# Sliding-window attention with the transposed probabilities as the stationary operand

## The chip, the core and the metric

The kernel runs on one NeuronCore of a Trainium2 chip. Five engines have instruction queues of their own: TensorE (PE, matmuls and transposes into PSUM), VectorE (DVE), ScalarE (ACT), GpSimd (POOL) and SyncE (SP, DMA issue). The metric is the device time of one execution, in microseconds, as the median of several runs.

## What is computed

Two layers over 1024 tokens of width 1024, all in float32. The first has two head groups behind one input projection: sliding-window softmax attention (8 query heads of 64, 2 key/value heads, window 128, a learned sink per head) and four DeltaNet heads. The second is a gated linear recurrence. Each mixer and each squared-relu MLP is followed by a layer norm. The part that the change touches is this one, per block of 128 queries and its band of 256 keys:

```
s = jnp.einsum('bnqhgd,bnkhd->bnhgqk', qb, kb).astype(f32) * (DH ** -0.5)
...
s = jnp.where(mask[None, :, None, None], s, -jnp.inf)
...
p = jax.nn.softmax(jnp.concatenate([s, sink], axis=-1), axis=-1)[..., :-1]
o = jnp.einsum('bnhgqk,bnkhd->bnqhgd', p.astype(v.dtype), vb)
```

## The kernel before

The tokens are two streams of 512 (c = 0 and 1), each in four blocks of 128 (n). Large products are made from split operands: every float32 matrix is written as a high part (fp32r, tiles `h`, `wh`) and a low part (`l`, `wl`), and `mm3` issues three matmuls. Their PSUM tiles are named `mm` (four banks). Everything small, such as attention, DeltaNet and the transposes of the layer norm, uses tiles named `mx` (four other banks). ACT and DVE make the high and low parts of the weights (`wblock`), which arrive in `ws`. `proj_fm` has weights stationary and activations moving (in the order `mm<-g,wh`), `proj_tm` the reverse.

The order on TensorE is fixed while the kernel is built, by a planner in Python (`Clock`, and the loop at the end of `trunk`). It keeps a planned time for every engine. The two streams yield the large products, and small chains (`attention`, `attn_preps`, `head_mid`, `layernorm`, called mixers) are put between them as soon as their operands are ready by the planned times. `Clock.matmul` charges a float32 matmul with 4 x 0.42 ns for each moving column, whatever the stationary operand is. `PE.last` chains all TensorE instructions, so their order on the chip is exactly the planned one. Instructions on the other engines are ordered by the compiler's scheduler.

`attn_block` handles one block n. It makes the scores (`mx<-kT,g`) with queries on partitions, adds the mask and takes the maximum (DVE), and exponentiates in place with the sum in `den` (ACT). Then it multiplies each of the eight probability tiles by one over its sum (ACT), transposes them on TensorE in groups of four, copies each group out of PSUM to `pT`, and multiplies: `v` (64 columns) is stationary, `pT` (512 columns) moves. One such product stands behind each group of transposes. The output already has channels on partitions and goes into `oT` through `split_ps`. The first block of stream 0 has one key tile instead of two.

Three conditions of the planner matter below. `attention` holds two granules of the pool `g` (`slot`) until the last block of stream 1 is done. `mix_out` of a stream (output projection, then layer norm) needs free granules, and its layer norm needs four more before its transposes are planned. And `mlp` chooses, at every second eighth of the hidden width, between two ways for W2: `straight` (eight products of quarter matrices for each fourth of the hidden width) and `weave`/`seven` (seven products, with sums of W2's quarters made earlier by DMA); stream 0 stays with `straight` until the output projection of stream 1 has been planned:

```
while e < 8 and not ((c == 1 or sts[1].get("op", -1) >= layer) and rings["g"] >= 2 and e % 2 == 0):
    if e == 7:
        res["start"]()
    yield from straight(e, e == 7)
    e += 1
```

Of the kernel before, what the change touches and what calls it, by code (L numbers as in the profile page):

```python
# [12 lines left out]
AF = mybir.ActivationFunctionType  # L13
ALU = mybir.AluOpType
# [3 lines left out]
P = 128  # L18
# [195 lines left out]
def trunk(ctx: ExitStack, tc, I, out):  # L214
    nc = tc.nc
    clk = Clock(tc, nc)
    V, G, S, PE = clk.engine(nc.vector, "V"), clk.engine(nc.gpsimd, "G"), clk.engine(nc.scalar, "S"), clk
    DS, DA, DG = clk.engine(nc.sync, "V"), clk.engine(nc.scalar, "V"), clk.engine(nc.gpsimd, "V")
    at = lambda *a: lambda: clk.ready(*a)
# [12 lines left out]
    def nm(s):  # L232
        uid[0] += 1
        return f"{s}_{uid[0]}"
# [34 lines left out]
    def wait(cond):  # L269
        while not cond():  # L270
            yield BLOCK
# [4 lines left out]
    def mx_ps():  # L276
        return clk.tile("mx", 4, pmx.tile([P, 512], F32, tag="mx", name=nm("mx")))

    def v4(a):
        return a.rearrange("p (a b) -> p a b", a=4)  # L280

    def bc_last(a, n):
        return a.unsqueeze(2).to_broadcast([P, a.shape[1], n])
# [9 lines left out]
    ident, U, M1 = C["ident"], C["U"], C["M1"]  # L293
# [100 lines left out]
    def split_ps(h, l, ps):  # L394
        S.copy(h, ps)
        V.tensor_tensor(l, ps, h, ALU.subtract)
# [419 lines left out]
    def attn_block(c, n, st, oT, tl, o):  # L816
        vr = st["v"][n]
        yield from wait(lambda: "ok" in o)
        qT, kT = o["qT"], o["kT"]
        pk, pv = att["kT"], att["v"]  # L820
        keys = ([(pk, pv)] if pk is not None else []) + [(kT, vr)]
        att["kT"], att["v"] = kT, vr
        k0 = 2 - len(keys)
        w = len(keys) * P
        sc = cpool.tile([P, 40], F32, tag="asc", name=nm("asc"), bufs=2)
        mx, nmx, den, es = (sc[:, i * 8:(i + 1) * 8] for i in range(4))
        pm = []
        for gp in range(2):
            yield lambda: max(clk.ready(qT, kT), clk.bank("mx", 4, 2))
            ps = [mx_ps().rearrange("p (g k) -> p g k", g=2) for _ in range(2)]  # L830
            for g2 in range(2):
                g = 2 * gp + g2
                for i, (kk, _) in enumerate(keys):
                    for h in range(2):
                        PE.matmul(ps[h][:, g2, i * P:(i + 1) * P], qT[h * 64:(h + 1) * 64, g * P:(g + 1) * P],
                                  kk[h * 64:(h + 1) * 64, :], start=True, stop=True)
            for h in range(2):
                pt = tl[2 + 2 * gp + h].rearrange("p (g k) -> p g k", g=2)
                for g2 in range(2):
                    i = 2 * (2 * gp + g2) + h  # L840
                    V.tensor_tensor_reduce(pt[:, g2, :w], ps[h][:, g2, :w], C["amask"][:, k0 * P:], 1.0, NEG,
                                           ALU.add, ALU.max, mx[:, i:i + 1])
                pm.append(pt)
        V.scalar_tensor_tensor(nmx, mx, -0.125, nsink, ALU.mult, ALU.min)
        V.tensor_tensor(es, W["sinks"], nmx, ALU.add)
        for m in range(4):
            for g2 in range(2):
                i = 2 * (2 * (m // 2) + g2) + m % 2
                S.activation(pm[m][:, g2, :w], pm[m][:, g2, :w], AF.Exp, bias=nmx[:, i:i + 1], scale=0.125,
                             accum_out=den[:, i:i + 1])  # L850
        S.activation(es, es, AF.Exp)
        V.tensor_tensor(den, den, es, ALU.add)
        V.reciprocal(den, den)
        for m in (0, 2, 1, 3):
            for g2 in range(2):
                i = 2 * (2 * (m // 2) + g2) + m % 2
                S.activation(pm[m][:, g2, :w], pm[m][:, g2, :w], AF.Copy, scale=den[:, i:i + 1])
        yield at(*pm)
        po = mx_ps()
        pend = None  # L860
        for i, (_, vv) in enumerate(keys):
            for h in range(2):
                ps = mx_ps()
                for g in range(4):
                    PE.transpose(ps[:, g * P:(g + 1) * P], pm[2 * (g // 2) + h][:, g % 2, i * P:(i + 1) * P], ident)
                pT = tl[(6, 7, 2, 3)[2 * i + h]]
                (S.copy if h else V.tensor_copy)(pT, ps)
                yield at(pT)
                PE.matmul(po[h * 64:(h + 1) * 64, :], vv[:, h * 64:(h + 1) * 64], pT, start=(i == 0),
                          stop=(i == len(keys) - 1))  # L870
        h, l = oT.quad(0, n)
        split_ps(h, l, v4(po))
        yield lambda: 0.0


# [377 lines left out]
    def attention(c, st, oT, o):  # L1253
        for n in range(NT):
            yield from attn_block(c, n, st, oT, slot["tl"], o[n])
            st["att"] = n + 1
        if c == 1:
            free("g", *slot["g"])
# [143 lines left out]
    while streams or mixers:  # L1402
        m = next((m for m in mixers if m[0]() + MARGIN <= clk.now), None) if clk.bank("mx", 4) <= clk.now else None
# [144 lines left out]
```

## Time and profile before

| | us |
|---|---|
| median of 3 runs (2270.96 to 2272.14) | 2271.65 |
| the profiled execution | 2273.03 |
| span of its instructions | 2271.3 |
| TensorE busy | 2210.8 (97%) |
| DVE busy | 1546.5 (68%) |
| ACT busy | 1049.1 (46%) |

The span runs from the first to the last instruction; 1.7 us of the profiled execution lie around it. Attention runs from about 100 to 440 us of the span. The output projection of stream 0 ends at 443 us, and from then to about 490 us its layer norm runs beside the DeltaNet chains of stream 1. The first product of `seven` starts at 803.9 us.

### The profile page before, as it was taken

What the parts mean: (1) busy time and instruction counts of PE and PEld (TensorE: products, weight loads), DVE (VectorE), ACT (ScalarE), POOL (GpSimd) and SP (SyncE); (2) the same over time, 40 slices, a digit from 0 to 9 for tenths busy, and PEclk for the clock granted to TensorE, in tenths of its full rate; (3) what the DMA queues carried; (4) which work ended last, traced back from release to release, by engine and by line L of the source; (5) the groups of instructions that cost most, each with busy time, mean ns of one, the idle gap of its engine ahead of it and who ended that gap; (6) DMA issues with size and microseconds to landing.
All of it is one profiled execution on the core that took longest, in us unless ns stands there. A gap on an engine that the chain in (4) does not pass through costs nothing.

```text
span 2271.3 us, 31951 instructions
## 1 busy us (share of the span) xinstructions
PE 2210.8 (97%) x12436; PEld 1787.7 (79%) x12436; DVE 1546.5 (68%) x2809; ACT 1049.1 (46%) x1878; POOL 28.9 (1%) x56
## 2 busy tenths in 40 slices
PE   8999999979999999999999999999999999999997
PEld 7767877757878887888888878778788887888886
DVE  7787776576555567586567898685565657776477
ACT  5465456244422344454444677373434444444442
POOL 0000000000000000000000000000000000000000
PEclk9999999999999999999999999999999999999999
DMA  4121223256677666677775333323523443444341
GB/s 168 59 78 39 94 77 115 81 171 185 192 200 225 207 215 199 208 255 222 232 216 184 130 130 129 122 75 102 181 98 127 140 144 128 150 169 145 122 165 66
DMA packets 89944, 337.46 MB, mean 149 GB/s; under 512 B 9920, under 2 KB 10304, under 8 KB 81600
## 3 DMA queue, kind: packets, MB, share of 16 engines
q1 hardware_dynamic: 76688, 280.56, 35.7%
q0 software_dynamic: 4608, 33.56, 7.8%
q10 hardware_dynamic: 8496, 21.30, 2.7%
q8 instruction: 97, 1.59, 0.3%
q14 instruction: 55, 0.45, 0.1%
HBM read 324.37 MB, written 78.12 MB: 177 GB/s over the span
## 4 chain that ended last, share of the span: by engine, by line
PE 86%; DVE 8%; ACT 4%; DMA 1%; issue 1%; SPq 0%; ACTq 0%; DVEq 0%
PE mm L206 67%; PE mx L206 17%; DVE g L178 2%; PE mx L210 2%; DVE wl L178 1%; DVE s L178 1%; ACT g L178 1%; DVE t L178 1%; DVE f L178 1%; ACT s L178 1%; ACT wh L178 1%; DMA parked<-r 1%; ACT t L178 1%; ACT f L178 0%; DMA f<-parked 0%
## 5 line engine op out<-in xcount | busy, mean ns | idle before, releaser
L206 PE MATMUL mm<-g,wh 128*128 128x512 f32 x2816 | 883.7, 395 | 2.4 <-ACT g L178 1.2
L178 DVE TENSOR_TENSOR wl<-ws,wh 128x1024 fp32r<-128x1024 f32 (+1 forms) x444 | 538.9, 1214 | 395.7 <-ACT wh L178 391.0
L178 ACT CAST wh<-ws 128x1024 fp32r<-128x1024 f32 (+1 forms) x356 | 371.4, 1043 | 685.2 <-PE mm L206 587.0
L206 PEld LDWEIGHTS mm<-g,wh 128*128 128x128 f32 x2816 | 520.3, 188 | 110.0 <-DVE g L178 3.1
L206 PE MATMUL mm<-g,wl 128*128 128x512 f32 x1408 | 549.6, 390 | 0.0
L206 PE MATMUL mm<-wh,s 128*128 128x512 f32 x1152 | 376.9, 394 | 0.7 <-DVE g L178 0.7
L206 PEld LDWEIGHTS mm<-g,wl 128*128 128x128 f32 x1408 | 264.6, 188 | 55.8
L206 PEld LDWEIGHTS mm<-wh,s 128*128 128x128 f32 x1152 | 217.0, 188 | 46.5 <-ACT s L178 1.1
L206 PE MATMUL mm<-wh,g 128*128 128x512 f32 (+1 forms) x768 | 239.7, 383 | 6.4 <-ACT wh L178 6.2
L206 PE MATMUL mm<-wl,s 128*128 128x512 f32 x576 | 225.1, 391 | 0.0
L206 PE MATMUL mx<-wh,s 128*128 128x512 f32 x576 | 188.0, 392 | 1.2 <-DVE s L178 1.2
L206 PEld LDWEIGHTS mm<-wh,g 128*128 128x128 f32 x768 | 142.9, 191 | 33.4 <-ACT wh L178 6.2
L178 ACT CAST s<-g 128x512 fp32r<-128x512 f32 x172 | 104.7, 622 | 105.5 <-PE mm L206 53.5
L178 DVE TENSOR_TENSOR s<-g,s 128x512 fp32r<-128x512 f32 x172 | 116.4, 688 | 45.0 <-ACT s L178 44.9
L206 PE MATMUL mm<-wl,g 128*128 128x512 f32 (+1 forms) x384 | 144.1, 375 | 0.4 <-DVE wl L178 0.4
L206 PEld LDWEIGHTS mx<-wh,s 128*128 128x128 f32 x576 | 108.2, 188 | 24.0 <-DVE s L178 2.0
L206 PEld LDWEIGHTS mm<-wl,s 128*128 128x128 f32 x576 | 108.6, 189 | 21.4 <-issue 0.2
L206 PE MATMUL mx<-wl,s 128*128 128x512 f32 x288 | 112.2, 390 | 0.0
L178 DVE CAST wh<-ws 128x1024 fp32r<-128x1024 f32 x88 | 60.5, 688 | 69.2 <-PE mm L206 62.4
L178 DVE TENSOR_TENSOR g<-g,mm 128x512 f32<-128x512 f32 x136 | 89.4, 684 | 13.4 <-PE mm L206 12.8
L178 ACT ACTIVATE g<-mm 128x512 f32<-128x512 f32 x100 | 59.1, 591 | 77.0 <-PE mm L206 77.0
L206 PEld LDWEIGHTS mm<-wl,g 128*128 128x128 f32 x384 | 73.3, 191 | 11.8 <-DVE wl L178 0.7
(234 smaller groups left out, 2397.3 us busy)
## 6 DMA issues: line engine op xcount, KB each, us to landing
ws<-w SPq DMA_DIRECT2D x232, 512.0 KB, 3.3
ws<-t SPq DMA_DIRECT2D x96, 512.0 KB, 3.4
t<-w POOLq DMA_DIRECT2D x32, 1024.0 KB, 9.0
ws<-hin_fm SPq DMA_DIRECT2D x32, 512.0 KB, 3.3
t<-w SPq DMA_DIRECT2D x16, 1024.0 KB, 7.1
t<-t SPq DMA_DIRECT2D x16, 1024.0 KB, 7.3
ws<-rin SPq DMA_DIRECT2D x32, 512.0 KB, 3.3
ws<-hout SPq DMA_DIRECT2D x16, 512.0 KB, 3.5
```

Source lines behind the costliest of these rows:

```text
L178: r = f(*a, **k)
L206: ins = self.pe.matmul(out, lhsT, rhs, start=start, stop=stop, skip_group_check=fresh)
L210: return self._pe(self.pe.transpose(out, x, ident), out, [x], 0.00042 * 2 * out.shape[-1])
```

## The change

The eight scalings of the probabilities on ACT are dropped. For each key/value head, the probabilities are transposed for both key tiles, and all four groups are copied out (`pT[i, h]`). Then, in one group of sixteen matmuls, 128 transposed probabilities of one query head are stationary and the 64 columns of `v` move; the output has query rows on partitions. One DVE instruction multiplies it by one over the sum (`y`), four transposes bring it to channels on partitions, and `split_ps` reads those.

```diff
-        for m in (0, 2, 1, 3):
-            for g2 in range(2):
-                i = 2 * (2 * (m // 2) + g2) + m % 2
-                S.activation(pm[m][:, g2, :w], pm[m][:, g2, :w], AF.Copy, scale=den[:, i:i + 1])
-        yield at(*pm)
-        po = mx_ps()
-        pend = None
-        for i, (_, vv) in enumerate(keys):
-            for h in range(2):
+        pT = {}
+        for h in range(2):
+            yield at(pm[h], pm[2 + h])
+            for i in range(len(keys)):
                 ps = mx_ps()
                 for g in range(4):
                     PE.transpose(ps[:, g * P:(g + 1) * P], pm[2 * (g // 2) + h][:, g % 2, i * P:(i + 1) * P], ident)
-                pT = tl[(6, 7, 2, 3)[2 * i + h]]
-                (S.copy if h else V.tensor_copy)(pT, ps)
-                yield at(pT)
-                PE.matmul(po[h * 64:(h + 1) * 64, :], vv[:, h * 64:(h + 1) * 64], pT, start=(i == 0),
-                          stop=(i == len(keys) - 1))
+                pT[i, h] = tl[(6, 7, 2, 4)[2 * h + i]]
+                (S.copy if i else V.tensor_copy)(pT[i, h], ps)
+                yield lambda: 0.0
+        yield at(*pT.values())
+        po = mx_ps()
+        for g in range(4):
+            for h in range(2):
+                o = po[:, (2 * g + h) * 64:(2 * g + h + 1) * 64]
+                for i, (_, vv) in enumerate(keys):
+                    PE.matmul(o, pT[i, h][:, g * P:(g + 1) * P], vv[:, h * 64:(h + 1) * 64], start=(i == 0),
+                              stop=(i == len(keys) - 1))
+        y = tl[3]
+        V.tensor_tensor(y.rearrange("p (i d) -> p i d", i=8), po.rearrange("p (i d) -> p i d", i=8), bc_last(den, 64),
+                        ALU.mult)
+        yield at(y)
+        ps = mx_ps()
+        for g in range(4):
+            PE.transpose(ps[:, g * P:(g + 1) * P], y[:, g * P:(g + 1) * P], ident)
         h, l = oT.quad(0, n)
-        split_ps(h, l, v4(po))
+        split_ps(h, l, v4(ps))
         yield lambda: 0.0
```

Since the planner sets the order, it moves other work too. In the rows below, a tile's name is followed by its number, `x4` counts equal instructions, and the output stands left of `<-`. TensorE, last attention block of stream 1, before (`csb` holds the identity, so those rows are transposes; `mm` rows are the output projection of stream 0):

```order
L206 MATMUL mx_4687<-g_147,vraw_3099 64x512
L210 MATMUL mx_4704<-csb,g_146 128x128 x2
L210 MATMUL mx_4704<-csb,g_147 128x128 x2
L206 MATMUL mm_4629<-wh_4671,g_1135 128x512
L206 MATMUL mm_4629<-wl_4672,g_1135 128x512
L206 MATMUL mm_4629<-wh_4671,g_1136 128x512
```

The same place in the changed kernel:

```order
L210 MATMUL mx_4400<-csb,g_146 128x128 x2
L210 MATMUL mx_4400<-csb,g_147 128x128 x2
L210 MATMUL mx_4406<-csb,g_146 128x128 x2
L210 MATMUL mx_4406<-csb,g_147 128x128 x2
L206 MATMUL mx_4412<-t_3404,t_3405 128x128
L206 MATMUL mx_4412<-t_3404,t_3447 128x128
L206 MATMUL mm_4164<-wh_4366,g_1363 128x512
L206 MATMUL mm_4164<-wl_4367,g_1363 128x512
L206 MATMUL mm_4164<-wh_4366,g_1365 128x512
```

The products with `v` no longer alternate with the transposes: sixteen of them (`mx_4423<-vraw_3055,g_147 128x64` and its like) follow three matmuls further down.

TensorE, layer norm of stream 0 (`mx<-csb,g` are its transposes, `mx<-t_4413` with 32x32 the DeltaNet chain of a head of stream 1), before:

```order
L206 MATMUL mx_5142<-t_4413 32x32 x16
L206 MATMUL mx_5161<-t_4413 32x32 x16
L210 MATMUL mx_5179<-csb,g_4291 128x128 x4
L206 MATMUL mx_5189<-t_4413 32x32 x16
L210 MATMUL mx_5208<-csb,g_4291 128x128 x4
L210 MATMUL mx_5218<-csb,g_4291 128x128 x4
L206 MATMUL mx_5225<-t_4413 32x32 x16
L210 MATMUL mx_5243<-csb,g_4291 128x128 x4
L206 MATMUL mm_5265<-g_4818,wh_5261 128x512
```

The layer norm of stream 0 in the changed kernel:

```order
L210 MATMUL mx_4930<-csb,g_4156 128x128 x4
L210 MATMUL mx_4940<-csb,g_4156 128x128 x4
L206 MATMUL mm_4914<-g_2041,wh_4910 128x512
L206 MATMUL mm_4914<-g_2042,wh_4910 128x512
L206 MATMUL mm_4914<-g_2041,wl_4911 128x512
L210 MATMUL mx_4950<-csb,g_4156 128x128 x4
L210 MATMUL mx_4978<-csb,g_4157 128x128 x4
```

Large products of stream 1 now stand between the transposes, and the 32x32 steps of the DeltaNet chain all come after them. From the end of the output projection to the last transposes of this layer norm the order has 96 large matmuls, seven 32x32 groups of sixteen and four other DeltaNet groups before, and 108 large matmuls, no 32x32 group and three other DeltaNet groups now.

TensorE, first MLP of stream 0: the first W2 product after those of the first two fourths of the hidden width (the rows ahead of it end a hidden block), before:

```order
L206 MATMUL mm_7876<-g_4821,wh_7872 128x512
L206 MATMUL mm_7876<-g_4820,wl_7873 128x512
L206 MATMUL mx_7903<-wh_7911,s_7905 128x512
L206 MATMUL mx_7903<-wl_7912,s_7905 128x512
L206 MATMUL mx_7903<-wh_7911,s_7906 128x512
```

The same product's beginning in the changed kernel:

```order
L206 MATMUL mm_7797<-g_4790,wh_7793 128x512
L206 MATMUL mm_7797<-g_4789,wl_7794 128x512
L206 MATMUL mm_7827<-wh_7833,s_7369 128x512
L206 MATMUL mm_7827<-wl_7834,s_7369 128x512
L206 MATMUL mm_7827<-wh_7833,s_7370 128x512
```

The output of W2 goes to an `mm` bank instead of an `mx` bank: `straight` stands where `seven` stood. Over the whole program TensorE has 32 transposes and 120 matmuls of 128x64 more, 30 products with `v` of 64x512 fewer, and 24 large matmuls more, since the third fourth of stream 0's first MLP is made with eight products (192 matmuls) instead of seven (168). In two stretches the order of TensorE is the same as before: the one that took about 880 to 1320 us in the trace before, and all from about 1606 us to the end.

## Rows read from the trace of the kernel before

**Rows 1.** Page, parts 1 and 2: busy time, and clock in 40 slices.

```profile
PE 2210.8 (97%) x12436; PEld 1787.7 (79%) x12436; DVE 1546.5 (68%) x2809; ACT 1049.1 (46%) x1878; POOL 28.9 (1%) x56
...
PE   8999999979999999999999999999999999999997
...
PEclk9999999999999999999999999999999999999999
```

**Rows 2.** Windows: stretch, its length, busy time of each engine, granted clock, DMA.

```profile
core 0: us, PE busy (x) PEld busy (x) DVE busy (x) ACT busy (x) POOL busy (x), PEclk, DMA share, GB/s
110.00:443.00 333.00, 323.44 (x2577) 240.69 (x2577) 233.90 (x674) 178.21 (x515) 0.60 (x6) 1.00 0.24 80
...
458.00:497.00 39.00, 27.02 (x371) 20.32 (x370) 33.47 (x64) 19.71 (x34) 0.00 (x0) 0.87 0.53 183
...
790.00:880.00 90.00, 90.00 (x398) 74.58 (x398) 52.64 (x60) 38.06 (x51) 3.29 (x4) 1.00 0.71 222
...
1320.00:1606.00 286.00, 278.46 (x1238) 228.43 (x1237) 211.19 (x320) 166.36 (x253) 0.20 (x2) 0.99 0.33 115
```

**Rows 3.** Waits of PE, 0 to 520 us: total us, times, longest.

```profile
PE mx L206 <- DVE t L178: 10.9, 6, 3.9
PE mm L206 <- ACT wh L178: 6.2, 1, 6.2
```

**Rows 4.** Timeline of PE, 440 to 512 us: start, length, what, idle before.

```profile
475.36 0.51 PE L206 MATMUL mx<-t 32*32 32x32 f32 x32 [2.61 <-DVE t L178]
479.76 0.65 PE L206 MATMUL mx<-t 32*32 32x32 f32 x32 [3.90 <-DVE t L178]
480.34 1.11 PE L210 MATMUL mx<-csb,g 128*128 128x128 f32 x4
...
486.73 0.50 PE L206 MATMUL mm<-g,wh 128*128 128x512 f32 x1 [1.17 <-ACT g L178]
```

**Rows 5.** Timeline of DVE, 430 to 488 us: the layer norm of stream 0.

```profile
441.15 1.37 DVE L178 SCALAR_TENSOR_TENSOR g<-g,mm 128x512 f32<-128x512 f32 x2 [1.73 <-PE mm L206]
...
463.26 1.90 DVE L178 TENSOR_TENSOR g<-g,s 128x512 f32<-128x512 f32 x3
...
473.21 0.69 DVE L178 TENSOR_TENSOR g<-g,s 128x512 f32<-128x512 f32 x1
...
476.41 1.22 DVE L178 TENSOR_TENSOR wl<-ws,wh 128x1024 fp32r<-128x1024 f32 x1
477.54 0.29 DVE L178 TENSOR_TENSOR t<-t,mx 128x128 f32<-128x128 f32 x1
```

**Rows 6.** Timeline of PE, 112 to 135 us.

```profile
117.75 1.07 PE L206 MATMUL mx<-g,vraw 128*64 128x512 f32 x2
118.76 0.66 PE L210 MATMUL mx<-csb,g 128*128 128x128 f32 x4
119.25 0.61 PE L206 MATMUL mx<-t,t 128*128 128x128 f32 x4
...
122.44 0.67 PE L206 MATMUL mx<-s,s 64*64 64x64 f32 x8
123.05 1.07 PE L206 MATMUL mx<-g,vraw 128*64 128x512 f32 x2
124.05 0.49 PE L206 MATMUL mx<-t,t 128*128 128x128 f32 x2
```

**Rows 7.** Timeline of PE around 31.6 us: float32 matmuls of 16 moving columns.

```profile
31.63 0.51 PE L206 MATMUL mx<-dsc,csb 128*128 128x16 f32 x4
31.99 0.71 PE L206 MATMUL mm<-g,wh 128*128 128x512 f32 x2
```

**Rows 8.** Timeline of PE, 440 to 512 us: float32 matmuls of 128 moving columns.

```profile
449.56 1.06 PE L206 MATMUL mx<-t 128*128 128x128 f32 x8
450.45 1.06 PE L206 MATMUL mx<-t,t 128*128 128x128 f32 x8
```

**Rows 9.** Groups of ACT by form, 85 to 440 us: busy us, mean ns, idle before.

```profile
L178 ACT ACTIVATE g<-g,asc 128x256 f32<-128x256 f32 x112 | 50.8, 497 | 11.6 <-DVE asc L178 11.6
```

**Rows 10.** Groups of DVE by form, whole span.

```profile
L178 DVE TENSOR_TENSOR g<-g,mx 128x512 f32<-128x512 f32 x64 | 41.9, 682 | 0.2 <-PE mx L206 0.2
```

## Prediction

> **What bounds the kernel now.** I read the page's first part first: TensorE is busy for 97% of the span, DVE for 68%, ACT for 46% [rows 1]. What decides is therefore TensorE's own work and its few holes; relief on ACT or DVE counts only where it closes a hole. The slices show where the holes are: the start, the stretch around 460 to 500 us, and the end [rows 1]. The windows give their sizes [rows 2]. From 110 to 443 us, where attention runs, TensorE is idle for 333.00 - 323.44 = 9.6 us. From 458 to 497 us it is idle for 39.00 - 27.02 = 12.0 us, and the granted clock is 0.87 there. From 790 to 880 us there is no hole: 398 matmuls in 90.00 us, so a large matmul costs 0.226 us there. The waits say who ends the holes: up to 520 us mostly DVE with tiles `t` (DeltaNet operands), 10.9 us in 6 times, against one wait of 6.2 us for ACT, the start [rows 3]. No wait in that answer is for the scaled probabilities.
>
> The hole at 458 to 497 us is the one to understand. The timeline shows TensorE waiting 2.61 and 3.90 us for DVE ahead of 32x32 matmuls, and four transposes that took 1.11 us instead of 0.66 [rows 4, 6]. The clock of 0.87 is a mean of the levels 2.4 and 1.2 GHz: 0.13 / 0.5 x 39 = 10 us at the lower one, after TensorE had been idle. DVE was full meanwhile: the layer norm of stream 0 went through it from 441.15 to 473.90 us, mixed with DeltaNet steps, gates and weight splits [rows 5]. TensorE had run out of large matmuls, since the next ones needed that layer norm; they began at 486.73 us [rows 4].
>
> **Term a: the product itself.** Removed are 30 products of two instructions each. From the start of one to the next instruction's start it is 118.76 - 117.75 = 1.01 us, and 124.05 - 123.05 = 1.00 us [rows 6]; together 30.2 us. Added are 120 matmuls, 240 instructions, with 128 stationary and 64 moving columns. The trace has none of that form. One with 128 stationary and 16 moving columns costs (31.99 - 31.63) / 4 = 0.090 us [rows 7], one with 128 and 128 (450.45 - 449.56) / 8 = 0.111 [rows 8]. So few moving columns hardly help; what seems to be paid is the loading of 128 stationary columns. Smaller in both operands, 64 and 64, it is (123.05 - 122.44) / 8 = 0.076 [rows 6]. I take 0.100, between the two forms with 128 stationary columns: 24.0 us; the ends are 18.2 and 26.6. Added too are 32 transposes, (119.25 - 118.76) / 4 = 0.12 us each [rows 6], 3.9 us. Term a is 24.0 + 3.9 - 30.2 = -2.3 us, from -8.1 to +0.3.
>
> The Trainium skill, page "TensorE: Matmul & The Clock Gate", section "LDWEIGHTS (loading the stationary operand)", speaks against the swap: a load takes columns / 1.2 ns, 107 ns for 128, however few columns then move. By it, as an estimate, the 240 loads take 25.7 us and term a is -0.6. The trace's 0.090 and 0.111 lie on both sides of it.
>
> ACT loses 64 scalings. Their groups of 128x256 average 497 ns, together with the exponentials [rows 9], so some 29 us of 178 in that stretch; ACT is idle for half of it [rows 2], and none of it is on the path: 0. DVE gets eight multiplications out of PSUM at 0.682 us [rows 10], 5.5 us. DVE is busy 70% of that stretch [rows 2], and large matmuls of the projections stand between the products, the multiplication and the transposes: 0, and a rival below if that cover fails. The reciprocal leaves the chain to the transposes; TensorE did not wait for it.
>
> **Term b: 24 more large matmuls.** The planner charges the new products 0.107 us (64 x 4 x 0.42 ns) where the trace promises about 0.2. By its times attention ends earlier, its two granules come free earlier, and stream 0's projection and MLP start earlier against stream 1's DeltaNet chains. So at the third fourth of the hidden width stream 1's output projection isn't planned yet, and `straight` replaces `seven`: 192 matmuls for 168. TensorE has no hole there [rows 2], so all count: 24 x 0.226 = +5.4 us. The DVE and ACT work of `seven` that goes with it was hidden. This term is certain within 0.5.
>
> **Term c: the hole at 458 to 497 us.** It costs 12.0 us of idle time and about 2 us of slower work: sixteen transposes at (1.11 - 0.66) / 4 = 0.11 us extra. In the changed order the DeltaNet steps stand behind the layer norm's transposes, not among them, and 108 large matmuls stand ahead of the last ones. What DVE has to do for the layer norm shrinks accordingly. Before it took 32.7 us. In DVE's new order nine DeltaNet and gate instructions of 0.60 us (463.26: three in 1.9), twelve small ones of about 0.25 and one weight split of 1.13 (477.54 - 476.41) no longer stand in that stretch, and 1.5 us of it had been idle [rows 5]: 5.4 + 3.0 + 1.1 + 1.5 = 11.0, which leaves 22 us, the last normalised half some 20 us after the projection's end. TensorE gets to the last transposes after 108 x 0.226 + 9 groups of transposes x 0.49 + 16 DeltaNet instructions x 0.111 = 24.4 + 4.4 + 1.8 = 30.6 us. So it shouldn't wait. Behind that the MLP's first block needs the last split, 17 DVE instructions later (two weight splits, nine of 0.60 us, six smaller: about 9 us, so 30 with some waiting), and TensorE reaches it after 15 more large matmuls and four transposes, at 34: only some 3 us of slack. Of the 14 us I therefore take back 11, and leave 3 for waits that appear elsewhere. Bounds: 14 if nothing waits, 0 if the same DVE work merely stops TensorE at other places. The 11 is nearer to the full hole because both sums are ahead, the first by 10 us.
>
> **Term d: the rest.** The holes of 9.6 us (attention's stretch) and 286.00 - 278.46 = 7.5 us (1320 to 1606 us) lie where the order changes; they come from DeltaNet and the recurrent layer, whose chains are as long as before. I take 0, within 4 us either way. Between (880 to 1320) and after (from 1606 us) the order is unchanged, and so is the time.
>
> **Sum.** -2.3 + 5.4 - 11 + 0 = -7.9 us. The profiled execution took 2273.03 us (span 2271.3), which gives 2265.1; the median was 1.4 us lower, so 2264 us.
>
> **The rivals.** (1) *The hole only moves.* DVE has nearly the same total work; if the chains that were put off stop TensorE later, or the 3 us of slack are not there, c is -3: -2.3 + 5.4 - 3 = 0, 2272 us. For it: the planner knows nothing of how the scheduler orders DVE. Against: behind the layer norm each 32x32 group has 9 large matmuls (2 us) as cover. Chance 0.22.
> (2) *Slower: the four copies become a gate.* Before, TensorE waited for one copy of one group at a time; now the sixteen products wait for all four copies, two of them on DVE, and the new transposes wait for DVE's multiplication. If a weight split (1.13 us) stands ahead on DVE at both points, TensorE, which runs in a fixed order, stops with all large matmuls queued behind. Eight blocks x 2 x 1.13 = +18 us; with the sum above 2282. It decides for slower from 12 us in all, 0.8 us a point. Against: 6 to 18 matmuls (1.4 to 4 us) stand ahead of most of these points. Chance 0.12.
> (3) *Much faster.* Term a at 0.076 us an instruction and the whole hole gone: -8.1 + 5.4 - 14 = -17, 2255 us. Against: loads of 128 columns never came so cheap. Chance 0.08.
> (4) *It does not do what it says:* the ACT scaling was hidden and the swap itself is worth nothing (a = 0); with c it is the forecast's neighbour, 2266, and is counted in it.
>
> **How the numbers follow.** The forecast has 0.58, with a range of its own of 2258 to 2268. A measurement of this kernel can tell about 0.2% (4.5 us) from no change, so faster means below 2267. Of the forecast 0.52 lies there, and all of rival 3: 0.60. Within 0.2%: 0.06 of the forecast, 0.18 of rival 1 and 0.02 of rival 2, 0.26. Slower: 0.04 of rival 1 and 0.10 of rival 2, 0.14. The range reaches from rival 3 to the upper side of rival 1: 2255 to 2274 us.
>
> **What would show it.** Term a: the new matmuls start 0.09 to 0.11 us apart, in groups of about 3.2 us. Term b: 24 more large matmuls, the first `seven` product later in the sequence. Term c: the stretch from the output projection's end to the MLP's start with a clock of 1.00 and under 3 us idle. Rival 2: waits of TensorE for `g` (the copies or the multiplication) between 110 and 440 us, well over 1 us each. I am wrong if the idle time of TensorE from 110 to 570 us has not fallen by about 8 us or more.

## The result, and the profile after

The changed kernel takes 2283.3 us (median of 4 runs, 2278.7 to 2287.7), the kernel before 2271.8 beside it: a ratio of 1.0045, with an interval of 1.0033 to 1.0056. It is slower by 11.5 us by the medians, 7.5 to 12.7 by the interval; the forecast was 2264 us and a range up to 2274. The profiled execution is the shortest of the four, 2278.7 us with a span of 2276.9, so its trace shows about half of the loss.

The page of the changed kernel, parts 1 and 2, answers to [rows 1]:

```profile
PE 2217.0 (97%) x12672; PEld 1820.7 (80%) x12672; DVE 1537.6 (68%) x2803; ACT 1015.4 (45%) x1802; POOL 28.5 (1%) x56
...
PE   8999999999999999999999999899999999999997
...
PEclk9999999999999999999999999999999999999999
```

ACT lost 34 us of work, TensorE got 6, and DVE lost 9. The 7 that stood around 460 to 500 us is gone from TensorE's slices, and an 8 has come in the recurrent layer, at 1423 to 1480 us. The windows are finer; these answer to [rows 2] (stretch, its length, busy time of PE, PEld, DVE, ACT and POOL, granted clock, DMA share, GB/s):

```profile
110.00:443.00 333.00, 322.61 (x2795) 269.70 (x2794) 250.69 (x730) 158.88 (x458) 0.60 (x6) 0.99 0.24 77
...
465.00:520.00 55.00, 47.84 (x477) 35.81 (x476) 28.80 (x50) 21.70 (x41) 1.73 (x3) 0.95 0.76 235
110.00:570.00 460.00, 442.45 (x3784) 364.83 (x3782) 331.38 (x898) 211.66 (x569) 5.84 (x14) 0.99 0.36 112
790.00:880.00 90.00, 90.00 (x399) 74.53 (x398) 33.58 (x37) 29.40 (x40) 2.47 (x3) 1.00 0.59 181
1320.00:1606.00 286.00, 272.90 (x1206) 223.29 (x1204) 207.28 (x315) 163.41 (x247) 0.20 (x2) 0.98 0.33 112
...
426.00:465.00 39.00, 39.00 (x202) 32.95 (x201) 35.00 (x83) 19.23 (x30) 0.94 (x1) 1.00 0.42 143
```

Stream 0's output projection now ends at 426 us, not 443. The 39 us behind it, where the forecast wanted the hole closed, are full: 39.00 of 39.00 us at a clock of 1.00. But a hole of 7.2 us stands right behind, at 465 to 520 us, with a clock of 0.95, while the DMA engines move 235 GB/s. And from 1320 to 1606 us the idle time grew from 7.5 us [rows 2] to 13.1. The same window of the kernel before, for the stretch that the prediction's last sign is about:

```profile
110.00:570.00 460.00, 437.41 (x3601) 331.01 (x3601) 323.32 (x888) 231.71 (x627) 4.20 (x12) 0.99 0.33 106
```

TensorE's idle time from 110 to 570 us fell from 22.6 us to 17.6, by 5 and not by the 8 or more that the prediction named: the sign of being wrong has come.

The waits of TensorE from 440 to 525 us, in total, times and longest, have one line only:

```profile
PE mx L206 <- DVE t L178: 7.2, 2, 4.3
```

So the hole behind the projection became smaller and comes later, yet the whole is slower. To see where, the table gives how long TensorE takes between the same instructions of its order (A: stream 0's output projection ends; B and C: begin and end of the stretch from about 880 to 1320 us whose order is the same; D: the last stretch of equal order begins, at about 1606 us). I worked it out from the traces by counting TensorE's instructions in order. The runs in its lower part are told below.

| | start of attention to A, A to B | both | B to C | C to D |
|---|---|---|---|---|
| before | 333.1, 437.1 | 770.2 | 439.5 | 286.9 |
| changed | 315.8, 454.2 | 770.0 | 437.8 | 294.3 |
| changed, run again | 316.5, 456.3 | 772.8 | 438.0 | 294.2 |
| changed, four straights | 316.0, 454.1 | 770.1 | 440.5 | 289.5 |
| changed, late sums | 314.8, 444.4 | 759.2 | 437.8 | 293.5 |
| changed, four straights, late sums (two runs) | 316.5, 438.3 and 313.2, 438.9 | 754.8, 752.1 | 438.9, 440.2 | 288.3, 289.6 |
| before, six straights | 333.1, 442.0 | 775.1 | 439.1 | 290.8 |
| before, early sums | 333.1, 443.2 | 776.3 | 439.2 | 288.7 |
| before, late sums | 333.0, 436.3 | 769.3 | 442.9 | 285.3 |

In the profiled run the first 880 us gave neither gain nor loss, and the recurrent stretch (C to D) lost 7.4 us.

**Who held TensorE at 471 us.** Three timelines of the changed kernel: TensorE, then ACT, then DVE (start, length, what, idle before and who ended it):

```profile
475.60 0.45 PE L206 MATMUL mx<-t 32*32 32x32 f32 x32 [4.34 <-DVE t L178]
...
517.72 0.80 PE L206 MATMUL mx<-t,t 128*128 128x128 f32 x2 [2.82 <-DVE t L178]
```

```profile
472.00 0.63 ACT L178 ACTIVATE f<-f 128x512 f32<-128x512 f32 x1 [5.36 <-DMA f<-parked]
...
515.90 0.72 ACT L178 ACTIVATE f<-f,sm 128x512 f32<-128x512 f32 x1 [4.86 <-DMA f<-parked]
```

```profile
472.66 0.69 DVE L178 SCALAR_TENSOR_TENSOR f<-f,f 128x512 f32<-128x512 f32 x1 [5.05 <-ACT f L178]
...
516.65 0.75 DVE L178 SCALAR_TENSOR_TENSOR f<-f,sm,f 128x512 f32<-128x512 f32 x1 [3.70 <-ACT f L178]
```

Each block has the first wait and then the second. Read from the last block to the first: DVE waits for ACT, ACT for a DMA `f<-parked`, and the `t` steps of the DeltaNet chain stand behind that on DVE, so TensorE waits for them. `parked` is a detail that the sections ahead of the prediction did not need: `park` (line 921) makes some of stream 1's DeltaNet projections ahead of time and writes them to DRAM, 256 KB each; `head_front` and `head_z` (lines 939 and 964) read them back, all through SyncE's queue. The same queue issues the first half of each of W2's sums (`w2_sums`, line 515: 1 MB, `t<-w` or `t<-t`); GpSimd issues the second half, an addition. The planner starts `w2_sums` when stream 0 has finished its first layer norm (line 1389, `spawn(w2_sums())`).

SyncE's queue, before (the first such copy and the reads around it), and then in the changed kernel:

```profile
479.95 5.93 SPq L178 DMA_DIRECT2D f<-parked  x3
485.94 0.61 SPq L178 DMA_DIRECT2D t<-w  x1
491.03 0.33 SPq L178 DMA_DIRECT2D f<-parked  x1
```

```profile
454.90 0.60 SPq L178 DMA_DIRECT2D t<-w  x1
...
464.13 0.33 SPq L178 DMA_DIRECT2D f<-parked  x1
...
480.50 0.33 SPq L178 DMA_DIRECT2D f<-parked  x1
480.88 0.51 SPq L178 DMA_DIRECT2D t<-w  x1
...
493.13 0.33 SPq L178 DMA_DIRECT2D f<-parked  x1
...
494.92 0.58 SPq L178 DMA_DIRECT2D f<-parked  x1
495.59 0.49 SPq L178 DMA_DIRECT2D t<-t  x1
...
502.75 5.44 SPq L178 DMA_DIRECT2D f<-parked  x2
```

Before, the sums began at 485.94 us and one read came after. Now they begin 31 us earlier, since stream 0 moved forward against stream 1, and six reads come after. The second wait has the same chain, with the read that SyncE issued second in the last row, at 507.87 us. How long these reads take is in the DMA issues from 440 to 800 us (queue, number, size, median us from issue to landing), before and then changed:

```profile
t<-w SPq DMA_DIRECT2D x9, 1024.0 KB, 7.1
...
f<-parked SPq DMA_DIRECT2D x7, 256.0 KB, 3.6
```

```profile
t<-w SPq DMA_DIRECT2D x10, 1024.0 KB, 7.5
...
f<-parked SPq DMA_DIRECT2D x7, 256.0 KB, 7.8
```

### The profile page after: what moved, and what is told of

The parts are those of the page before. It is cut to its first block, busy times and chain, and to the rows that moved or that the text cites. A ratio compares the mean times of both kernels' runs of the same rounds, so it can differ in the third digit from the quotient of the medians.

```text
span 2276.9 us, 32320 instructions
## 1 busy us (share of the span) xinstructions
PE 2217.0 (97%) x12672; PEld 1820.7 (80%) x12672; DVE 1537.6 (68%) x2803; ACT 1015.4 (45%) x1802; POOL 28.5 (1%) x56
## 4 chain that ended last, share of the span: by engine, by line
PE 88%; DVE 6%; ACT 3%; DMA 2%; issue 1%; DVEq 0%; ACTq 0%; SPq 0%
PE mm L206 69%; PE mx L206 17%; DVE g L178 2%; PE mx L210 2%; DVE wl L178 1%; DVE s L178 1%; ACT wh L178 1%; DVE t L178 1%; DMA f<-parked 1%; ACT t L178 1%; DVE f L178 1%; ACT s L178 0%; ACT g L178 0%; ACT f L178 0%; DMA parked<-r 0%
## 5 line engine op out<-in xcount | busy, mean ns | idle before, releaser
L178 DVE TENSOR_TENSOR wl<-ws,wh 128x1024 fp32r<-128x1024 f32 (+1 forms) x438 | 530.8, 1212 | 392.7 <-ACT wh L178 388.9
L178 ACT CAST wh<-ws 128x1024 fp32r<-128x1024 f32 (+1 forms) x350 | 365.1, 1043 | 691.5 <-PE mm L206 596.6
L206 PE MATMUL mx<-wh,s 128*128 128x512 f32 x528 | 172.7, 392 | 1.8 <-DVE s L178 1.8
L178 ACT CAST s<-g 128x512 fp32r<-128x512 f32 x158 | 96.4, 623 | 101.5 <-PE mm L206 53.1
L178 DVE TENSOR_TENSOR s<-g,s 128x512 fp32r<-128x512 f32 x158 | 106.7, 686 | 41.0 <-ACT s L178 40.7
L206 PEld LDWEIGHTS mx<-wh,s 128*128 128x128 f32 x528 | 99.1, 188 | 23.2 <-DVE s L178 3.1
L178 DVE TENSOR_TENSOR g<-g,mm 128x512 f32<-128x512 f32 x144 | 95.0, 683 | 19.6 <-PE mm L206 19.1
L206 PE MATMUL mx<-wl,s 128*128 128x512 f32 x264 | 102.8, 389 | 0.0
L206 PE MATMUL mx<-g,wh 128*128 128x512 f32 x256 | 79.3, 391 | 0.0
```

The source lines that it names most:

```text
L178: r = f(*a, **k)
L206: ins = self.pe.matmul(out, lhsT, rhs, start=start, stop=stop, skip_group_check=fresh)
```

## The experiments

The first theory after the result put the loss on the two more `straight` passes; its rival put it on the new attention, or on something at its place. The first three runs take one part away each way, and run the changed kernel once more.

**Four straights.** The third fourth of stream 0's first MLP goes back to `seven`; the rest of the change stays.

```diff
-        while e < 8 and not ((c == 1 or sts[1].get("op", -1) >= layer) and rings["g"] >= 2 and e % 2 == 0):
+        while e < 8 and not ((c == 1 or (e == 4 if layer == 0 else sts[1].get("op", -1) >= layer)) and rings["g"] >= 2 and e % 2 == 0):
```

> The changed kernel, with the first MLP of stream 0 made to leave straight after four eighths, as before, not after six. TensorE's order is the changed kernel's up to that point, and the old kernel's from the start of the recurrent stretch to the end. Theory P (the attention and its re-planned surroundings gain about 7 us by 880 us, and the loss is all in the 24 extra matmuls and in the recurrent stretch, whose order they shift): about 2265 us, a ratio to the kernel before near 0.997, all runs within some 3 us. Theory A (the new attention product, or something at its place that the fastest profiled run doesn't show, is slow and makes the runs spread): still above 2272 us, about 2278 less 5 for the matmuls = 2273 to 2282, with the same spread of 8 us or so.

Measured: 2276.9 us (2266.8 to 2281.0, 11 runs), ratio 1.0016 (1.0005 to 1.0026). That is in theory A's range, though with a wider spread. Six microseconds come back, but the kernel is still slower than before, with waits of 5.82 and 6.25 us on TensorE at 472 and 497 us, behind parked tiles again: ahead of the first wait the write of the tile to DRAM took 8.1 us and its read followed, ahead of the second the read took 8.3.

**Six straights in the kernel before.** The same line in the kernel before, with 6 for 4.

> The kernel before, attention untouched, made to stay with straight for six eighths in the first MLP of stream 0. TensorE's order is the old one up to there, and nearly the changed kernel's in the recurrent stretch. Theory P: the old attention with the new recurrent stretch is slower than both, 2271.8 + 5.4 for 24 matmuls + about 7 in the recurrent stretch = 2284 us or more, with a spread like the changed kernel's. Theory A: only the 24 matmuls, 2277 us, and a narrow spread.

Measured: 2281.3 us (2280.2 to 2283.6), ratio 1.0041 (1.0028 to 1.0053), between the two theories. Two more straights alone cost the old kernel 9 us, not 5.4: 4.9 between A and B, and 3.9 between C and D. The second part is a single wait that the shifted order makes in the recurrent layer. TensorE of the changed kernel, and then of this one:

```profile
1477.90 1.11 PE L210 MATMUL mx<-csb,g 128*128 128x128 f32 x4 [6.29 <-DVE g L178]
```

```profile
1480.37 1.11 PE L210 MATMUL mx<-csb,g 128*128 128x128 f32 x4 [6.29 <-DVE g L178]
```

The windows of the changed kernel there show DVE full, and the clock that it costs behind the wait:

```profile
1440.00:1480.00 40.00, 33.62 (x150) 27.58 (x149) 37.74 (x81) 24.90 (x37) 0.00 (x0) 0.96 0.27 92
1480.00:1520.00 40.00, 38.53 (x169) 30.97 (x169) 30.42 (x43) 29.00 (x46) 0.00 (x0) 0.92 0.21 66
```

With four straights no such wait is there, with either attention (the longest of TensorE from 1320 to 1606 us are 2.9 and 3.1 us). So it belongs to the two straights.

**The changed kernel once more**, unedited.

> The changed kernel once more, for a second trace. If its runs differ by where the recurrent stretch waits, the stretch that took 1320 to 1606 us before is again several us longer, and the stretch up to 880 us takes within 1 us of the same time as in the first trace; if the spread comes from attention, the difference lies before 440 us.

Measured: 2282.0 us in its one run, with waits of 4.77 and 3.29 us at the same two places. The recurrent stretch is as long as in the first trace, but the stretch up to 880 us is not within 1 us: it takes 2.8 us more, 2.1 of them behind A, where these two waits are.

The two straights thus explain some 8 us of a loss against a gain that was forecast at 13, but with four of them the changed kernel still loses. What was left was the chain behind the parked reads. Three kernels move the sums and leave TensorE's order as it is.

**Four straights, late sums.** On top of the first edit:

```diff
-            spawn(w2_sums())
+            spawn(w2_sums(), clk.now + 60.0)
```

> The changed kernel with four straight eighths (as in the first of these experiments) and the DMA sums of W2's quarters started 60 planned us later; TensorE's order is the same as in that experiment, instruction for instruction. Theory D (the layer norm's hole did not close because the sums, 1 MB transfers, now run while the parked projections of stream 1 are read back; ACT waits for those reads, DVE for ACT, TensorE for DVE): the two waits of 5.8 and 6.3 us at 471 and 497 us shrink to under 3 us together, the time falls by about 10 us to 2263 to 2268, and the runs spread by less than 4 us. Theory O (the waits come from the new order alone, DVE's queue): no change, 2277 us with the same spread.

Measured: 2259.5 us (2256.4 to 2261.7), ratio 0.9935 (0.9923 to 0.9948). TensorE's order is that of the first experiment, instruction for instruction, and the time is 17 us lower, below theory D's range; the spread, 5.3 us, is wider than its 4. Of the two waits 0.8 us is left. The table says where the time went: from A to B it is 438.3 us for 454.1, and within 2 us the same elsewhere. The order on DVE and ACT, which the compiler makes anew, is no rival: it is the same in both kernels up to 505 us, behind both waits.

**The changed kernel with late sums**, the same edit alone.

> The changed kernel as it is (six straight eighths), with the sums started 60 planned us later; TensorE's order unchanged. Theory D: some 7 us less than the changed kernel's 2279 to 2287, about 2274, since its two waits there were 4.3 and 2.8 us in the trace of its fastest run and more in the others; the longer recurrent stretch stays. Theory O: 2279 to 2287 again.

Measured: 2267.3 us (2263.4 to 2270.6), ratio 0.9973 (0.9962 to 0.9984): 16 us below the changed kernel, in the same order, where theory D had only 7 (it had priced the waits by the shortest of the runs). Its windows at the place of the hole:

```profile
458.00:497.00 39.00, 38.37 (x436) 28.84 (x435) 26.21 (x49) 19.09 (x35) 0.00 (x0) 1.00 0.55 183
465.00:520.00 55.00, 54.37 (x509) 42.52 (x497) 34.71 (x61) 23.09 (x47) 0.10 (x1) 1.00 0.47 155
```

**The kernel before with early sums.** They start at the end of stream 0's output projection, some 47 us earlier.

```diff
+        if r == "s" and which == 0:
+            spawn(w2_sums())
...
-            spawn(w2_sums())
+            pass
```

> The kernel before, with the sums started at the end of stream 0's output projection, about 40 us earlier; TensorE's order unchanged. Theory D: the old kernel gets the same trouble, parked reads land in 5 us or more instead of 2.7, and it becomes 3 to 12 us slower with a wider spread. Theory O: 2272 us, within 2.

Measured: 2279.8 us (2276.4 to 2281.7), ratio 1.0028 (1.0018 to 1.0038). The old kernel gets the same trouble, by theory D's amount. TensorE, and ACT ahead of it:

```profile
483.59 0.65 PE L206 MATMUL mx<-t 32*32 32x32 f32 x32 [10.12 <-DVE t L178]
```

```profile
477.47 0.63 ACT L178 ACTIVATE f<-f 128x512 f32<-128x512 f32 x1 [7.49 <-DMA f<-parked]
```

**Later transposes of stream 0's layer norm**, in the changed kernel, to see if its new order among them is to blame.

```diff
+    calls = [0]
...
+        calls[0] += which == 2
+        done0 = which == 2 and calls[0] > 1
...
-                yield late(2.5, ytile(yg, n)[:, i * 512:(i + 1) * 512])
+                yield late(8.0 if which == 2 and r == "t" and not done0 else 2.5, ytile(yg, n)[:, i * 512:(i + 1) * 512])
```

> The changed kernel; only the transposes of stream 0's layer norm in the recurrent stretch are planned 8 us behind their operands' planned time, not 2.5, so that large matmuls stand ahead of them. If the single wait of 6.3 us at 1472 us, with the lower clock behind it, is what makes that stretch 7 us longer than before, the stretch falls by 6 to 9 us and the kernel to about 2272 to 2279. If the DVE work just stops TensorE elsewhere, the stretch falls by less than 3 us.

Measured: 2283.7 us (2281.4 to 2286.5), ratio 1.0048 (1.0032 to 1.0063). No gain: from C to D it takes 297.0 us, with a wait of 9.05 us in place of the 6.29. ACT ends it, having itself waited 7.73 us for DVE: DVE's work there stops TensorE at one place or another.

What the attention itself is worth needs the kernel before with the same late sums, on the same chip.

**The kernel before with late sums**, TensorE's order unchanged.

> The kernel before (old product with v, seven in its old place) with the sums of W2's quarters held back by 60 us of planned time; TensorE's order is that of the kernel before. It tells how much of the 12 us that the run with four straights and late sums gained is the attention, and how much the sums. Theory (the holes of the kernel before at 458 to 497 us come from VectorE, full with the layer norm and the DeltaNet steps; its parked tiles landed in time): little changes, 2268 to 2273 us, so the attention is worth 9 to 13 us once the sums are late, as terms a and c of the forecast said (-13.3). Rival (the sums hurt the kernel before as well): 2258 to 2263 us, so the attention's change gains nothing even with late sums, and terms a and c were wrong.

Measured: 2273.8 us (2272.1 to 2279.7), ratio 1.0007 (0.9998 to 1.0016), just above the theory's range and far from the rival's. Its windows answer to [rows 2] line for line, hole and clock included:

```profile
458.00:497.00 39.00, 27.86 (x381) 20.93 (x380) 33.74 (x65) 19.69 (x36) 0.10 (x1) 0.87 0.45 156
```

So the old hole was not the sums' doing, and holding them back is worth nothing there.

**A planner that charges the new products 0.215 us**, with four straights and late sums.

```diff
+        if n == 64 and lhsT.shape[-1] == P and rhs.dtype == F32:
+            c = 0.00042 * P * 4
```

> Changed attention, four straights, late sums, and the planner charges the 128x64 products 0.215 us instead of 0.107; TensorE's order differs from the run with four straights and late sums only between 110 and about 490 us. Theory (only the sums and the two straights cost anything; the price sets where attention's products stand, among enough large products in either case): 2256 to 2263 us, the same as without the price. Rival (the planner's too low price makes TensorE wait in attention): 3 to 8 us faster, 2251 to 2256 us, with fewer waits between 110 and 440 us.

Measured: 2266.2 us (2264.8 to 2270.6), ratio 0.9973 (0.9961 to 0.9984). Neither expectation held: the truer price is 7 us slower. It moves attention's pieces again, and TensorE waits for DVE at new places, 3.62 us at 161 us and 1.89 us at 458 us among them. A better number for one cost did not make a better order here; that the order on DVE, which isn't planned, is the whole reason is not shown.

**Four straights, late sums, again**, on the chip of the last two.

> The kernel with changed attention, four straights and late sums once more, on the same chip as the kernel before with late sums, so that the two differ by the attention alone. Theory: 2256 to 2262 us, 9 to 13 us below the kernel before with late sums. Rival: level with it within 3 us.

Measured: 2259.3 us (2257.2 to 2259.9), ratio 0.9937 (0.9923 to 0.9950), 14.5 us below the kernel before with late sums, a little more than the 9 to 13 expected. This is the version that beats both kernels. Its windows at the two places of the holes:

```profile
458.00:497.00 39.00, 37.41 (x432) 27.93 (x431) 25.78 (x48) 18.26 (x32) 0.00 (x0) 1.00 0.41 135
465.00:520.00 55.00, 53.41 (x493) 41.61 (x493) 33.16 (x61) 22.59 (x46) 0.10 (x1) 1.00 0.35 115
110.00:570.00 460.00, 448.18 (x3948) 369.97 (x3946) 337.13 (x910) 213.55 (x572) 3.38 (x11) 1.00 0.30 97
```

Two last kernels asked by what the sums delay the reads: as neighbours in SyncE's queue (Q), or in the DMA engines and the memory, whoever issues them (M).

**The sums' copies issued by GpSimd**, in the changed kernel.

```diff
-                yield behind(8.0 + 4.0 * layer, DS, layer, j, k, 0)
+                yield behind(8.0 + 4.0 * layer, DG, layer, j, k, 0)
```

> The changed kernel with one edit: the first half of each of W2's sums, a 1 MB copy, is issued by GpSimd (which issues the second half already) and no longer by SyncE, where the reads of the parked tiles are issued. TensorE's order is that of the changed kernel. It asks by what the sums delay those reads. Theory Q (they share SyncE's queue, and a read queued behind a 1 MB copy comes late): the longest landing of a read falls from 8.3 us to below 6, and the time to 2265 to 2272 us. Theory M (they share the DMA engines and the memory, whichever engine issues them): the longest landing stays at 7 to 10 us, and the time at 2277 to 2286 us.

Measured: 2269.2 us (2268.4 to 2271.1), ratio 0.9988 (0.9979 to 0.9997), longest landing of a read 6.4 us. The time is Q's, the landing neither theory's, and the edit did more than it should. GpSimd's timeline:

```profile
204.01 0.83 POOL L178 DMA_DIRECT2D t<-w  x1 [10.01 <-DMA t<-t]
...
513.12 0.10 POOL L178 MEMSET f<- 128x3 f32 x1 [308.28 <-DVE f L178]
513.57 0.54 POOL L178 DMA_DIRECT2D t<-t  x1 [0.34 <-issue]
```

The first sums went out at 176 to 204 us, and then a memset that waits for DVE held GpSimd, and all sums behind it, until 513 us. No sum ran beside the parked reads. So this is one more kernel with the sums out of the way, and no test between Q and M. Its slowest read ran beside four reads of `x` of 512 KB each, issued by ACT.

**The parked reads issued by ScalarE**, in the changed kernel.

```diff
-                DS.dma_start(raw[:, 3:515], parked[b])
+                DA.dma_start(raw[:, 3:515], parked[b])
...
-            DS.dma_start(ps, parked[b])
+            DA.dma_start(ps, parked[b])
```

> The changed kernel with one edit: the reads of the parked tiles are issued by ScalarE and no longer by SyncE; the sums stay where they were. TensorE's order is that of the changed kernel. Theory Q (the reads wait in SyncE's queue behind the sums): longest landing below 6 us, time 2265 to 2274 us; a read that waits on ScalarE for its tile to be written can hold up ScalarE's own work, which would take some of it back. Theory M (shared DMA engines and memory): longest landing 7 to 10 us, time 2277 to 2290 us.

Measured: 2286.3 us (2282.9 to 2287.9), ratio 1.0056 (1.0040 to 1.0073), longest landing 9.1 us. DMA issues from 440 to 800 us:

```profile
f<-parked ACTq DMA_DIRECT2D x7, 256.0 KB, 5.5
```

On a queue of their own the reads still land late, 5.5 us where they took 3.6 before. That is M. Since ScalarE issues each of them later, behind its own work, the time itself decides less.

The trace of the changed kernel says the same of its two waits. GpSimd's additions there start when the copy ahead of them on SyncE's queue has landed:

```profile
462.65 0.94 POOL L178 DMA_DIRECT2D t<-w  x1 [286.92 <-DMA t<-w]
...
506.01 0.81 POOL L178 DMA_DIRECT2D t<-w  x1 [14.83 <-DMA t<-t]
```

The reads behind the two waits were issued after that, at 464.13 and 507.87 us, with no copy of the sums under way on SyncE's queue. They took 7.8 and 7.9 us to land, and ACT went on at 472.00 and 515.90. The additions, on GpSimd's queue, took 9.0 and 9.5 us from issue to landing, and each read came in within 0.4 us behind its addition. So these reads came late beside the additions, and not for a place behind a copy in SyncE's queue. The sums are not the only transfers that can do it: with late sums in the changed kernel one read took 6.9 us beside four reads of `x` of 512 KB, and TensorE waited 0.63 us. Whether the shared thing is the DMA engines or the memory stays open.

## Why the prediction was wrong

The whole loss, added up from medians: the sums of W2 held back in the kernel before, +1.2 us (2272.6 to 2273.8); the attention and the order that it makes, with four straights and late sums on both sides, -14.5 (to 2259.3); two more straights, +8.0 (to 2267.3); sums at their own early time, +16.0 (to 2283.3). Together +10.7; the medians of the first comparison give +11.5. The last step compares two chips; taken against the kernel before beside each, it is +17.2.

**Term a** was off by 2 to 3 us, at the edge of its range. One block's products in the changed kernel:

```profile
388.82 3.68 PE L206 MATMUL mx<-vraw,g 128*128 128x64 f32 x32
392.34 0.66 PE L206 MATMUL mx<-S,t 128*128 128x128 f32 x4
```

(392.34 - 388.82) / 32 = 0.110 us; over all eight blocks 26.7 us for 240, 0.111 each. I had taken 0.100, between the forms of 16 and of 128 moving columns; it is that of 128 columns [rows 8]. The 0.090 was read wrongly: it is the mean of four steps from start to start [rows 7], of which the first is 0.027 us and the other three are 0.111 to 0.112. The 0.076 of 64 and 64 [rows 6] is such a mean too; six of its eight steps are 0.058 to 0.059 us, and the two at the ends are longer. So with 128 stationary columns 16, 64 and 128 moving ones all cost 0.111, and there was no range to choose from. With the transposes, 3.2 to 3.9 us, and 30.1 us removed, term a is between -0.2 and +0.5: the swap itself gives nothing, so the 14.5 us do not come from the product itself. The estimate by the Trainium skill, page "TensorE: Matmul & The Clock Gate", section "LDWEIGHTS (loading the stationary operand)", 0.107 us a load, came nearer than my choice between two rows; the trace agrees with it to 4%.

**ACT and DVE.** ACT's scalings went as told; no wait in [rows 3] was for them, and no run takes them out alone. Rival 2, the four copies as a gate, did not come: from 110 to 443 us TensorE is idle for 10.4 us against 9.6, and of its waits there those for `g` on DVE and ACT are 1.8 us together. That this rival's 2282 us is near the measured time is chance.

**Term b** was right in its mechanism and its count (24 more large matmuls, no hole to hide them: 4.9 us between A and B in the old kernel). It was short by what the shift does later, the wait of 6.29 us in the recurrent layer, which I had put into term d as 0 within 4. Between C and D the two straights cost 3.9 us in the old attention and 3.9 to 5.2 in the new; over the whole kernel 9.0 and 8.0, where term b had 5.4.

**Term c** was right where it was worked out. DVE's layer norm ran from 424.27 to 447.13 us, and TensorE came to its last transposes at 456.02:

```profile
446.45 0.68 DVE L178 TENSOR_TENSOR g<-g,s 128x512 f32<-128x512 f32 x1
...
456.02 0.60 PE L210 MATMUL mx<-csb,g 128*128 128x128 f32 x4
```

The first is 22.9 us where I had 22, the second 29.7 us after the projection's end where I had 30.6, and nothing waited in between. With the sums out of the way the idle time from 110 to 570 us falls from 22.6 us to 11.8 (448.18 busy of 460 in the best kernel), by the 11 that I took. Terms a and c together were -13.3; the attention with late sums measured -14.5. That they come so near is partly luck: term a gave 2 to 3 us less, and in the traces the stretch up to B gained 17.2 us, the one from B to C 2.7, and the one from C to D gave 4.3 back (the last row of the table against the second run with four straights), which no term had.

**The step that failed** is the end of term c: "leave 3 for waits that appear elsewhere", with its price worked out from TensorE and DVE alone. What moves with stream 0's layer norm is also what is started behind it. I had followed the order of TensorE and DVE, and not the DMAs: on SyncE's queue the first 1 MB copy of the sums moved from behind all but one of the parked reads to ahead of six of them, and the additions that follow on GpSimd's queue now run beside these. In place of 3 us this cost 16 to 17, as the runs with late sums show. Rows of the kernel before would have shown both halves: copies that take 7.1 us beside reads that take 3.6, and a read that ACT, DVE and TensorE wait for in turn. ACT and DVE there, ahead of the wait of 3.90 us in [rows 4]:

```profile
478.04 0.63 ACT L178 ACTIVATE f<-f 128x512 f32<-128x512 f32 x1 [3.94 <-DMA f<-parked]
...
478.70 0.69 DVE L178 SCALAR_TENSOR_TENSOR f<-f,f 128x512 f32<-128x512 f32 x1 [0.87 <-ACT f L178]
```

Rival 1 (the hole only moves) had the right place, "elsewhere", but the wrong cause and no room for a time above 2272: the new wait is not the old DVE work, since DVE is idle for 5.05 us in it.

The range failed for the same reason. Its upper end came from c = -3, so it held no case in which the moved step makes a wait that was not there.

## What to carry to other kernels

When a change shifts one stream of work against another, list what is spawned at the shifted moment, its DMAs first, and look, over all DMA queues together, for the short reads that they now run beside. A large background transfer should start after the short reads that a chain waits for, not when the program happens to reach it: here one number moved the result from 0.45% slower to 0.27% faster, and to 0.6% faster once the choice of W2's product was held as well. And try the timing of such a transfer before judging the change that moved it.

## What the runs showed that was not expected

A 256 KB read from DRAM landed in 3.6 us (median) where all but one came before the 1 MB copies, in 7.8 us where six of seven came among the copies and additions, and in 5.5 us when another engine's queue issued it there; of the sums, the two that TensorE came to wait for had only an addition of GpSimd's queue beside them, and no copy of their own queue. With 128 stationary columns a float32 matmul of 16, 64 or 128 moving columns costs 0.111 us an instruction. And the truer cost in the planner made the kernel 7 us slower, with new waits of TensorE for DVE, whose order the planner doesn't set.
